# Output norms in steps behind later slots, and two more banks for the down units: a decoder layer on one Trainium2 core

## The chip, the cores and the metric

One core of one Trainium2 chip runs the kernel. Its engines are TensorE (PE, with its weight loads PEld), VectorE (DVE), ScalarE (ACT), GpSimd (POOL) and SyncE (SP); SP issues nearly all DMAs. The metric is device time in microseconds (us), the median of several runs. Before the change it is 2489.42 us, the median of 3 runs from 2483.08 to 2493.25.

## The reference

One layer of a decoder is computed for a prompt of 2048 positions and for 8 samples of 4 positions, all in float32, model width 1024:

```
z = rmsnorm(x) @ w_in                      # q, k, v for 8 heads; u, v for 8 gated groups
mix = [dilated window attention | u * spatial gate]
x = x + mix @ w_out
h = rmsnorm(x)
x = x + (silu(h @ w_gate) * (h @ w_up)) @ w_down      # hidden width 2816
y = rmsnorm(x)                                         # returned, with key and value windows
```

The change concerns the last two lines: the product with `w_down` and the final norm `y = x / sqrt(mean(x^2) + eps) * final_g`, which needs a whole row of 1024 values before any value of it can be scaled.

## The kernel before

The order of the instructions on every engine is the order in which the program writes them; nothing reorders them. A float32 product is made of three matmuls on a high and a low part of each operand (`hh*wh`, `hh*wl`, `hl*wh`), so each operand tile is first split: ACT copies the high part (L1883 and L1884), DVE subtracts it for the low part (L1885 and L1886).

The prompt's 16 row tiles of 128 go through the first half of the layer in three blocks of 6, 6 and 4 tiles. The hidden width is 22 slices of 128. Behind each block stand **down units** (`first_downs` L1785, `down_unit` L1780): the products of the last two slices with `w_down`, for one row tile each, in two halves of 512 columns and six matmuls a half (L1776). Each half fills a PSUM bank, and DVE adds that bank to the row tile (L1778, L1799). Before the change all units take their banks from `ps_o`, which hands out two banks by turns; `ps_t` hands out two others, used for transposes and gates elsewhere. Behind the units come the next block's products with `w_out` and its norm.

The other 20 slices of `w_down` are multiplied at the end, in the **second part** (class `Down`). They form 10 pairs (NJ), and the product is done as a seven-product block scheme in two halves of the rows (`hv` 0 and 1). Each product `s` (0 to 6) runs over the 10 pairs `j`, and one step `n` of these 2 x 7 x 10 = 140 is called a **slot**: `n = 70 hv + 10 s + j`. A slot has 12 matmuls of 512 columns, for four row groups `m` into four banks. Its program text, in order: `tick()` (work that `later(k, ...)` put k slots on), operand sums of slot n+3 on DVE (only for products 1 to 5), the split of slot n+3 on ACT and DVE, the loads of slot n+6 on SP, the matmuls, and in slots j = 0 to 3 the eviction (L1920) of one bank of the product before into the row tiles `acc[i]`. Operand tiles are a ring of 8 (two a slot), so the split of slot n+3 can start when the matmuls of slot n-1 are done. Weight tiles are a ring of 10. SP issues in order too: a store that waits for its row holds up the loads behind it. The last three slots (TAIL) are done at the end in the order of the row groups: for each `m` the 9 matmuls of slots 137 to 139, then its eviction.

Which half rows are finished when follows from `EVICTS`: the even row tiles get their first 512 columns complete with product 1 and the rest with product 5, the odd ones their second 512 columns with product 4 and the rest with product 6. So the **final norms** come in three places: for even rows behind product 5 (evicted from slots 60 and 130 on), for odd rows of `hv` 0 behind product 6 (from slot 70 on), for odd rows of `hv` 1 in the tail. `final_a` (L1808) squares the whole row on ACT; one slot later `rms_b` (L1457, L1458) forms mean and root; two slots later `final_b` (L1815) does the Newton step (L146 to L150) and the scaling of the whole row on DVE (L1818); three slots later SP issues the store. These steps stand in `tick()`, ahead of the slot's own split. Only the odd rows of `hv` 1 have a prepared half: `square_half` (L1950) squares it and multiplies it by the gain on POOL (L1955).

Of the kernel before, what the change touches and what calls it, by code (L numbers as in the profile page):

```python
# [10 lines left out]
F32 = mybir.dt.float32  # L11
F32R = mybir.dt.float32r
AF = mybir.ActivationFunctionType
OP = mybir.AluOpType
# [52 lines left out]
def hymba_step(ctx: ExitStack, tc: tile.TileContext, A: dict, O: dict):  # L67
# [26 lines left out]
    def ps_o():  # L94
        turn[1] ^= 1
        return bank(2 + turn[1])
# [81 lines left out]
    def zn_tile():  # L178
        return rp.tile([P, 512], F32, name="zn", tag="zn", bufs=3)
# [1597 lines left out]
                          stop=(z == FC - 1 and y == len(pairs) - 1))  # L1777
        dve.tensor_add(B.acc[i][0:nr, cs], B.acc[i][0:nr, cs], ps[0:nr])  # L1778

    def down_unit(B, i, h):  # L1780
        tick()
        for half in range(2):
            down_half(B, i, h, half, ps_o())

    def first_downs(B, i0, i1, h):  # L1785

# [39 lines left out]
    class Down:  # L1826
# [92 lines left out]
            x = self.acc[hv * 8 + 2 * m + q][:, cs]  # L1919
            dve.tensor_add(x, x, banks[m])  # L1920

        def final(self, i):
            final_a(self.acc[i], O["yp"][i * P:(i + 1) * P, :])

        def run(self):
            for n in range(2 * NS - TAIL):
                hv, s, j = self.at(n)
                tick()
                self.sums(n + 3)
                self.split(n + 3)  # L1930
                self.load(n + 6)
                if s in (0, 2) and j in (5, 8):
                    self.acc_loads(hv, s // 2, j // 8)
                if s > 2 and n % 2 == 0 and n < NS + 5 * NJ:
                    roll(1)
                self.mats(n)
                if n >= NJ and j < 4:
                    phv, ps_, _ = self.at(n - j - 1)
                    self.evict(phv, ps_, j, self.prev)
# [10 lines left out]
        def square_half(self, m):  # L1950

            x = self.acc[8 + 2 * m + 1][:, 512:]
            self.sq[m] = s1 = self.p2.tile([P, 4], F32, name="sq", tag="sq", bufs=4)
            act.activation(zn_tile(), x, AF.Square, accum_out=s1[:, 3:4])
            pool.tensor_mul(x, x, gain[1][:, 512:])  # L1955

        def tail(self):
            n0 = 2 * NS - TAIL
            for _ in range(4):
                tick()  # L1960

            def finish(m):
                i = 8 + 2 * m + 1
                x, s1 = self.acc[i], self.sq[m]
                rms_b(s1, P, s1[:, 3:4])
                r = rms_c(s1, P)
                act.activation(x[:, 512:], x[:, 512:], AF.Copy, scale=r)
                dve.scalar_tensor_tensor(x[:, 0:512], x[:, 0:512], r, gain[1][:, 0:512], op0=OP.mult, op1=OP.mult)
                for z in (1, 0):
                    sync.dma_start(O["yp"][i * P:(i + 1) * P, z * 512:(z + 1) * 512], x[:, z * 512:(z + 1) * 512])  # L1970
# [262 lines left out]
    for bi, B in enumerate(blocks):  # L2233
# [188 lines left out]
```

## Time and profile before

The profiled execution took 2493.14 us, with a span of 2491.4 us from the first to the last instruction; the median of the runs is 2489.42.

| engine | busy, us | share of the span |
|---|---|---|
| PE | 2397.9 | 96% |
| PEld | 2120.8 | 85% |
| DVE | 1691.0 | 68% |
| ACT | 1211.9 | 49% |
| POOL | 1183.7 | 48% |

How to read it: PE's busy time is a union of overlapping matmuls, so what counts is how far apart their starts are. The second part's matmuls start 0.227 us apart when nothing holds them, 2.72 us a slot. A row of the timeline gives start, length (us), engine, line, operation, the tiles written and read, the count where rows were merged, and in brackets how long the engine was idle before it and what ended that. Tile names are cut: `op` are split operands, `ac` and `acc` row tiles, `ps_m`, `ps_t`, `ps_o` banks, `fr` weight tiles.

### The profile page before, as it was taken

The page shows a single profiled execution, that of the slowest core. Times are in us where ns is not written, and L with a number is a line of the kernel's source. Part 1 is how long each engine was busy: PE and PEld are TensorE (multiplying, and loading weights), DVE is VectorE, ACT ScalarE, POOL GpSimd, SP SyncE. Part 2 cuts the span into 40 slices and gives each one's busy share as a digit, 9 for nine tenths or more (in the row PEclk, how much of TensorE's full clock was granted, in tenths as well). Part 3 has the DMA queues.
Part 4 walks back from the last instruction along what each step waited for, and adds up shares of the span by engine and source line. Part 5 has one row for each costly group of instructions (what it writes and reads, how often), then busy time and mean ns, then how long its engine had stood idle before and what let it go on. Part 6 is the DMA issues. An engine that isn't in the chain of part 4 may idle for free. (4 is left out here: it accounts for less than half of the span.)

```text
span 2491.4 us, 39127 instructions
## 1 busy us (share of the span) xinstructions
PE 2397.9 (96%) x13358; PEld 2120.8 (85%) x13358; DVE 1691.0 (68%) x3081; ACT 1211.9 (49%) x2385; POOL 1183.7 (48%) x909
## 2 busy tenths in 40 slices
PE   8999999999989889999999999999999999999997
PEld 6787777778888777999998899999799998887886
DVE  4368686446878777656655776776566666877876
ACT  6414344546877656433333633334455554445444
POOL 1145643224575746666663576666467881000000
PEclk9999999999999999999999999999999999999999
DMA  8863854788788665566659177666647776755832
GB/s 265 255 202 112 275 147 140 246 278 265 232 281 259 218 185 171 190 212 207 202 200 320 36 250 255 231 243 226 255 151 229 234 221 235 279 186 197 318 128 89
DMA packets 315221, 537.17 MB, mean 216 GB/s; under 512 B 28417, under 2 KB 151714, under 8 KB 309134
## 3 DMA queue, kind: packets, MB, share of 16 engines
q1 hardware_dynamic: 310060, 526.16, 64.6%
q10 hardware_dynamic: 4962, 8.51, 1.3%
q8 instruction: 106, 1.74, 0.3%
q14 instruction: 93, 0.76, 0.1%
HBM read 418.41 MB, written 186.28 MB: 243 GB/s over the span
## 5 line engine op out<-in xcount | busy, mean ns | idle before, releaser
L1686 PE MATMUL ps_m<-xh,op 128*128 128x384 f32 (+5 forms) x1932 | 612.3, 317 | 0.8 <-DVE raw L1714 0.5
L1687 PE MATMUL ps_m<-xl,op 128*128 128x384 f32 (+5 forms) x1932 | 612.0, 317 | 0.0
L1688 PE MATMUL ps_m<-xh,op 128*128 128x384 f32 (+5 forms) x1932 | 611.3, 316 | 0.0
L1623 POOL TENSOR_TENSOR op<-fr,op 128x512 fp32r<-128x512 f32 x286 | 402.6, 1424 | 91.7 <-ACT op L1619 65.0
L1686 PEld LDWEIGHTS ps_m<-xh,op 128*128 128x128 f32 x1932 | 363.9, 188 | 2.4 <-issue 0.8
L1687 PEld LDWEIGHTS ps_m<-xl,op 128*128 128x128 f32 x1932 | 363.8, 188 | 0.6
L1688 PEld LDWEIGHTS ps_m<-xh,op 128*128 128x128 f32 x1932 | 364.2, 188 | 0.0
L1623 POOL TENSOR_TENSOR op<-pair,op 128x512 fp32r<-128x512 f32 x126 | 169.6, 1347 | 158.3 <-DVE hr L1748 87.1
L1619 ACT ACTIVATE op<-fr 128x512 fp32r<-128x512 f32 x330 | 196.6, 621 | 12.2 <-PE ps_m L1438 6.0
L335 PE MATMUL ps_s<-wh,xh 128*128 128x512 f32 x480 | 195.8, 408 | 6.1 <-ACT xh L139 6.1
L336 PE MATMUL ps_s<-wl,xh 128*128 128x512 f32 x480 | 189.9, 396 | 0.0
L337 PE MATMUL ps_s<-wh,xl 128*128 128x512 f32 x480 | 189.5, 395 | 0.1
L1737 ACT ACTIVATE ps_t<-zn 128x384 f32<-128x384 f32 (+2 forms) x132 | 60.0, 454 | 250.4 <-DVE zn L1716 205.5
L1883 ACT ACTIVATE op<-fr 128x512 fp32r<-128x512 f32 x140 | 88.3, 631 | 173.9 <-issue 89.2
L1955 POOL TENSOR_TENSOR ac<-ac,final_g 128x512 f32<-128x512 f32 x2 | 2.6, 1296 | 351.9 <-DMA fr<-t_d 349.3
L1885 DVE TENSOR_TENSOR op<-fr,op 128x512 fp32r<-128x512 f32 x140 | 99.3, 710 | 80.4 <-ACT op L1883 80.1
L1619 ACT ACTIVATE op<-pair 128x512 fp32r<-128x512 f32 x126 | 79.0, 627 | 110.9 <-DVE pair L1609 110.9
L335 PEld LDWEIGHTS ps_s<-wh,xh 128*128 128x128 f32 x480 | 91.5, 191 | 34.5 <-issue 7.3
L1900 PE MATMUL ps_m<-op 128*128 128x512 f32 x280 | 109.0, 389 | 0.9 <-ACT op L1884 0.9
L1902 PE MATMUL ps_m<-op 128*128 128x512 f32 x280 | 109.1, 390 | 0.2
L337 PEld LDWEIGHTS ps_s<-wh,xl 128*128 128x128 f32 x480 | 91.5, 191 | 20.8 <-POOL xl L142 0.5
L1901 PE MATMUL ps_m<-op 128*128 128x512 f32 x280 | 109.0, 389 | 0.0
(551 smaller groups left out, 5942.0 us busy)
## 6 DMA issues: line engine op xcount, KB each, us to landing
fr<-in_w_gate_dram SPq DMA_DIRECT2D x132, 256.0 KB
out_ks_dram<-in_cache_k_dram SPq DMA_DIRECT2D x56, 512.0 KB
out_vs_dram<-in_cache_v_dram SPq DMA_DIRECT2D x56, 512.0 KB
fr<-in_w_up_dram SPq DMA_DIRECT2D x110, 256.0 KB
fr<-ab_d SPq DMA_DIRECT2D x88, 256.0 KB
a<-h_d SPq DMA_DIRECT2D x80, 256.0 KB
fr<-t_d SPq DMA_DIRECT2D x80, 256.0 KB
raw<-in_w_in_dram SPq DMA_DIRECT2D x72, 256.0 KB
```

Source lines behind the costliest of these rows:

```text
L335: pe.matmul(o[j], xh[:, k, :], wh, start=(k == 0), stop=False)
L336: pe.matmul(o[j], xh[:, k, :], wl, start=False, stop=False)
L337: pe.matmul(o[j], xl[:, k, :], wh, start=False, stop=(k == KD - 1))
L1619: act.activation(ops[f, j][0], ab[f][j], AF.Copy)
L1623: (eng or pool).tensor_sub(lo_, ab[f][j], hi.bitcast(F32))
L1686: pe.matmul(out, wh[:, ks], xh[:, :, k], start=(k == 0), stop=False)
L1687: pe.matmul(out, wh[:, ks], xl[:, :, k], start=False, stop=False)
L1688: pe.matmul(out, wl[:, ks], xh[:, :, k], start=False, stop=(k == 3))
L1885: dve.tensor_sub(wl, w, wh.bitcast(F32))
L1900: pe.matmul(banks[m], hh[:, ts], wh, start=first, stop=False, skip_group_check=more)
L1901: pe.matmul(banks[m], hh[:, ts], wl, start=False, stop=False, skip_group_check=more)
L1902: pe.matmul(banks[m], hl[:, ts], wh, start=False, stop=j == NJ - 1, skip_group_check=more)
```

## The change

Four things change.

1. Down units behind blocks 0 and 1 take their banks from `ps_t` and `ps_o` by turns; in front of the second part the units of the sample rows and of tile 3 take `ps_t`, the one of tile 2 `ps_o`.
2. Evictions: in all products but the last one of `hv` 1 they are written in slots j = 0, 2, 4, 6 instead of 0, 1, 2, 3.
3. Final norms: each row tile's first finished half is prepared early (`early_half`, behind products 1 and 4): one slot after its eviction ACT squares it and POOL multiplies it by the gain. Behind products 5 and 6 (`late_half`) six steps follow at the ends of later slots, 1 to 6 slots on: square of the other half (ACT), mean (DVE), root (ACT), Newton step and scaling of the half (DVE), scaling of the prepared half by a copy (ACT), two stores of a half row each (SP). In the last product of `hv` 1 the steps are 1, 2, 2, 3, 3, 4 slots on, with evictions in slots j = 0 to 3.
4. Tail: steps still queued are written out ahead of its matmuls; mean, root and Newton step of group m-1 stand ahead of the eviction of group m instead of behind it.

```diff
--- before.py
+++ after.py
@@ down units @@
-    def down_unit(B, i, h):
+    def down_unit(B, i, h, place=None):
         tick()
         for half in range(2):
-            down_half(B, i, h, half, ps_o())
+            down_half(B, i, h, half, (place or ps_o)())
@@ in class Down @@
-        def final(self, i):
-            final_a(self.acc[i], O["yp"][i * P:(i + 1) * P, :])
+        def behind(self, k, fn, *args):
+            self.queue.setdefault(self.n + k, []).append((fn, args))
+
+        def square(self, i, c):
+            x = self.acc[i][:, c * 512:(c + 1) * 512]
+            act.activation(zn_tile(), x, AF.Square, accum_out=self.sq[i][:, (0, 3)[c == i % 2]:][:, 0:1])
+
+        def early_half(self, i):
+
+            self.sq[i] = self.p2.tile([P, 4], F32, name="sq", tag="sq", bufs=8)
+            c = i % 2
+            x = self.acc[i][:, c * 512:(c + 1) * 512]
+            self.behind(1, self.square, i, c)
+            self.behind(1, pool.tensor_mul, x, x, gain[1][:, c * 512:(c + 1) * 512])
+
+        def late_half(self, i, quick=False):
+            steps = (1, 2, 2, 3, 3, 4) if quick else (1, 2, 3, 4, 5, 6)
+            for k, fn in zip(steps, (self.late_square, self.mean, self.root, self.scale, self.scale_rest, self.out)):
+                self.behind(k, fn, i)
+
+        def late_square(self, i):
+            self.square(i, 1 - i % 2)
+
+        def mean(self, i):
+            s1 = self.sq[i]
+            dve.tensor_scalar(s1[:, 0:1], s1[:, 0:1], s1[:, 3:4], None, op0=OP.add)
+            dve.tensor_scalar(s1[:, 1:2], s1[:, 0:1], 1.0 / D, EPS, op0=OP.mult, op1=OP.add)
+
+        def root(self, i):
+            act.activation(self.sq[i][:, 2:3], self.sq[i][:, 1:2], AF.Sqrt)
+
+        def scale(self, i):
+            r = rms_c(self.sq[i], P)
+            cs = slice((1 - i % 2) * 512, (2 - i % 2) * 512)
+            x = self.acc[i][:, cs]
+            dve.scalar_tensor_tensor(x, x, r, gain[1][:, cs], op0=OP.mult, op1=OP.mult)
+
+        def scale_rest(self, i):
+            x = self.acc[i][:, i % 2 * 512:(i % 2 + 1) * 512]
+            act.activation(x, x, AF.Copy, scale=self.sq[i][:, 2:3])
+
+        def out(self, i):
+            for c in (i % 2, 1 - i % 2):
+                cs = slice(c * 512, (c + 1) * 512)
+                sync.dma_start(O["yp"][i * P:(i + 1) * P, cs], self.acc[i][:, cs])
...
                 self.mats(n)
-                if n >= NJ and j < 4:
+                wide = not (hv and s == 6)
+                m = j // 2 if wide else j
+                if n >= NJ and m < 4 and not (wide and j % 2):
                     phv, ps_, _ = self.at(n - j - 1)
-                    self.evict(phv, ps_, j, self.prev)
-                    if ps_ == 5:
-                        self.final(phv * 8 + 2 * j)
-                    if ps_ == 6:
-                        self.final(phv * 8 + 2 * j + 1)
-                    if hv == 1 and s == 5:
-                        self.square_half(j)
+                    self.evict(phv, ps_, m, self.prev)
+                    i = phv * 8 + 2 * m
+                    if ps_ in (1, 4):
+                        self.early_half(i + ps_ // 4)
+                    elif ps_ in (5, 6):
+                        self.late_half(i + ps_ - 5, not wide)
+                for fn, args in self.queue.pop(n, ()):
+                    fn(*args)
...
         def tail(self):
             n0 = 2 * NS - TAIL
             for _ in range(4):
                 tick()
+            for n in sorted(self.queue):
+                for fn, args in self.queue[n]:
+                    fn(*args)
...
             for m in range(4):
                 for n in range(n0, 2 * NS):
                     self.mats(n, (m,))
+                if m:
+                    begin(m - 1)
+                    r[m - 1] = root_end(m - 1)
                 self.evict(1, 6, m, self.Y)
-                act.activation(zn_tile(), self.acc[8 + 2 * m + 1][:, 0:512], AF.Square, accum_out=self.sq[m][:, 0:1])
+                self.late_square(8 + 2 * m + 1)
                 if m:
-                    finish(m - 1)
-            finish(3)
+                    finish(m - 1, r[m - 1])
+            begin(3)
+            finish(3, root_end(3))
@@ in second_part: units of the sample rows and of tile 3; unit 2 stays @@
-        down_unit(B, m, h)
+        down_unit(B, m, h, ps_t)
...
-        down_unit(B, 3, h)
+        down_unit(B, 3, h, ps_t)
@@ behind blocks 0 and 1 @@
-            downs += [lambda B=B, pair=pair, i=i: down_unit(B, i, pair) for i in last[2:]]
+            downs += [lambda B=B, pair=pair, i=i, p_=p_: down_unit(B, i, pair, p_) for i, p_ in zip(last[2:], (ps_t, ps_o) * 2)]
```

On PE, the down units behind block 0 (`ps_o`, `ps_t` and `ps_m` are the kinds of banks, `dw` the weights, `hw` the hidden values):

```order
 L1797 MATMUL ps_m_14044<-dw,hw 128x512 x3
-L1776 MATMUL ps_o_14098<-dw,hw 128x512 x6
-L1776 MATMUL ps_o_14106<-dw,hw 128x512 x6
+L1776 MATMUL ps_t_14098<-dw,hw 128x512 x6
+L1776 MATMUL ps_t_14106<-dw,hw 128x512 x6
 L1776 MATMUL ps_o_14115<-dw,hw 128x512 x6
 L1776 MATMUL ps_o_14123<-dw,hw 128x512 x6
-L1776 MATMUL ps_o_14139<-dw,hw 128x512 x6
-L1776 MATMUL ps_o_14147<-dw,hw 128x512 x6
+L1776 MATMUL ps_t_14139<-dw,hw 128x512 x6
+L1776 MATMUL ps_t_14147<-dw,hw 128x512 x6
```

No matmul has moved; every second unit writes the other pair of banks.

On DVE, behind product 5 of `hv` 0, before the change (from a slot's split to the next slot's eviction; `s` holds a row's mean and root):

```order
L1885 TENSOR_TENSOR op<-fr_24073,op 128x512
L1886 TENSOR_TENSOR op<-a_23178,op 128x512
L1920 TENSOR_TENSOR ac<-ac,ps_o_23441 128x512
L146 RECIPROCAL s_24135<-s_24135 128x1
L148 TENSOR_SCALAR s_24135<-s_24135 128x1
L149 TENSOR_SCALAR s_24135<-s_24135 128x1
L150 TENSOR_SCALAR s_24135<-s_24135 128x1
L1818 SCALAR_TENSOR_TENSOR ac<-ac,s_24135,final_g 128x1024
L1457 TENSOR_SCALAR s_24167<-s_24167 128x1
L1885 TENSOR_TENSOR op<-fr_24093,op 128x512
L1886 TENSOR_TENSOR op<-a_23202,op 128x512
L1920 TENSOR_TENSOR ac<-ac,ps_o_23442 128x512
```

and in the changed program (`sq` holds mean and root):

```order
L1920 TENSOR_TENSOR ac<-ac,ps_o_23457 128x512
L146 RECIPROCAL sq<-sq 128x1
L148 TENSOR_SCALAR sq<-sq 128x1
L149 TENSOR_SCALAR sq<-sq 128x1
L150 TENSOR_SCALAR sq<-sq 128x1
L1957 SCALAR_TENSOR_TENSOR ac<-ac,sq,final_g 128x512
L1947 TENSOR_SCALAR sq<-sq 128x1
L1948 TENSOR_SCALAR sq<-sq 128x1
L1885 TENSOR_TENSOR op<-fr_24169,op 128x512
L1886 TENSOR_TENSOR op<-a_23255,op 128x512
L1885 TENSOR_TENSOR op<-fr_24193,op 128x512
L1886 TENSOR_TENSOR op<-a_23281,op 128x512
```

Between two evictions there are now two slots' splits instead of one, and the scaling is of half a row.

On ACT, in the last slots before the tail, before the change (L1811 squares a whole row, L1458 is the root, L1883 and L1884 are a slot's split):

```order
L1811 ACTIVATE pair,s_25868<-acc_18451 128x1024
L1458 ACTIVATE s_25868<-s_25868 128x1
L1883 ACTIVATE op<-fr_25796 128x512
L1884 ACTIVATE op<-a_24899 128x512
L1811 ACTIVATE pair,s_25900<-acc_18535 128x1024
L1458 ACTIVATE s_25900<-s_25900 128x1
```

and in the changed program (L1961 is the copy of the prepared half, L1951 the root, L1927 the square of half a row):

```order
L1961 ACTIVATE ac<-ac,sq 128x512
L1951 ACTIVATE sq<-sq 128x1
L1927 ACTIVATE zn,sq<-acc_18451 128x512
L1883 ACTIVATE op<-fr_25881 128x512
L1884 ACTIVATE op<-a_24973 128x512
L1961 ACTIVATE ac<-ac,sq 128x512
L1951 ACTIVATE sq<-sq 128x1
L1927 ACTIVATE zn,sq<-acc_18535 128x512
```

Root and square still stand between two slots' splits, now behind them in the program's slot, with a copy added.

More of the change, by code (lines that the diff above doesn't have):

```diff
@@ L1920, in evict @@
             dve.tensor_add(x, x, banks[m])
-        def final(self, i):
-            final_a(self.acc[i], O["yp"][i * P:(i + 1) * P, :])
+        def behind(self, k, fn, *args):
[33 more added lines that the diff above has]
+                sync.dma_start(O["yp"][i * P:(i + 1) * P, cs], self.acc[i][:, cs])
         def run(self):
+            self.queue = {}
             for n in range(2 * NS - TAIL):
+                self.n = n
                 hv, s, j = self.at(n)
@@ L1948, in run @@
             self.tail()
[L1950 to L1955, printed above, removed]
         def tail(self):
@@ L1960, in tail, with begin, root_end, finish @@
                 tick()
-            def finish(m):
+            for n in sorted(self.queue):
+                for fn, args in self.queue[n]:
+                    fn(*args)
+            def begin(m):
                 i = 8 + 2 * m + 1
-                x, s1 = self.acc[i], self.sq[m]
-                rms_b(s1, P, s1[:, 3:4])
-                r = rms_c(s1, P)
+                self.mean(i)
+                self.root(i)
+            def root_end(m):
+                return rms_c(self.sq[8 + 2 * m + 1], P)
+            def finish(m, r):
+                i = 8 + 2 * m + 1
+                x = self.acc[i]
                 act.activation(x[:, 512:], x[:, 512:], AF.Copy, scale=r)
                 dve.scalar_tensor_tensor(x[:, 0:512], x[:, 0:512], r, gain[1][:, 0:512], op0=OP.mult, op1=OP.mult)
-                for z in (1, 0):
-                    sync.dma_start(O["yp"][i * P:(i + 1) * P, z * 512:(z + 1) * 512], x[:, z * 512:(z + 1) * 512])
+                self.out(i)
+            r = {}
             for m in range(4):
```

## The prediction

> **What bounds the kernel now.** I read the stages first, then the starts of TensorE's matmuls, then what DVE and ACT do where those starts spread. The windows of the second part (us; then busy us of PE, PEld, DVE, ACT, POOL; granted clock; DMA share; GB/s):
>
> ```profile
> 2113.00:2250.00 137.00, 137.00 (x606) 113.46 (x605) 106.91 (x172) 58.96 (x102) 0.00 (x0) 1.00 0.64 218
> 2250.00:2306.00 56.00, 51.58 (x216) 39.88 (x216) 42.12 (x90) 28.97 (x59) 0.00 (x0) 1.00 0.67 226
> 2306.00:2440.00 134.00, 134.00 (x592) 110.96 (x591) 108.29 (x170) 58.94 (x106) 5.18 (x4) 1.00 0.60 212
> 2440.00:2475.00 35.00, 31.87 (x130) 24.96 (x129) 24.97 (x51) 17.14 (x35) 0.00 (x0) 0.95 0.19 70
> 2475.00:2491.40 16.40, 4.59 (x21) 3.46 (x19) 9.22 (x31) 5.54 (x14) 0.00 (x0) 0.79 0.34 128
> ```
>
> TensorE is full except in 2250-2306, in 2440-2475 and after it: where the norms of the output rows run. How much is lost there, from first matmuls of slots (0, 65, 76, 80):
>
> ```profile
> 2085.47 0.40 PE L1900 MATMUL ps_m<-op 128*128 128x512 f32 x1
> ...
> 2262.28 0.39 PE L1900 MATMUL ps_m<-op 128*128 128x512 f32 x1
> ...
> 2296.19 0.50 PE L1900 MATMUL ps_t<-op 128*128 128x512 f32 x1 [1.53 <-ACT op L1884]
> ...
> 2310.35 0.39 PE L1900 MATMUL ps_m<-op 128*128 128x512 f32 x1
> ```
>
> Slots 0 to 65 take 176.81 us, 2.72 each. The 15 slots from 65 to 80 take 48.07 where 40.80 would do: **7.27 us lost**. TensorE waits for split operands (ACT op). One norm slot on DVE, and ACT between:
>
> ```profile
> 2295.64 0.69 DVE L1885 TENSOR_TENSOR op<-fr,op 128x512 fp32r<-128x512 f32 x1 [0.79 <-ACT op L1883]
> ...
> 2296.86 0.68 DVE L1920 TENSOR_TENSOR ac<-ac,ps_m 128x512 f32<-128x512 f32 x1
> 2297.45 0.16 DVE L146 RECIPROCAL s<-s 128x1 f32<-128x1 f32 x1
> ...
> 2298.39 1.29 DVE L1818 SCALAR_TENSOR_TENSOR ac<-ac,s,final_g 128x1024 f32<-128x1024 f32 x1
> 2299.59 0.15 DVE L1457 TENSOR_SCALAR s<-s 128x1 f32<-128x1 f32 x1
> 2300.53 0.69 DVE L1885 TENSOR_TENSOR op<-fr,op 128x512 fp32r<-128x512 f32 x1 [0.79 <-ACT op L1883]
> ```
>
> ```profile
> 2299.77 0.20 ACT L1458 ACTIVATE s<-s 128x1 f32<-128x1 f32 x1 [0.99 <-DVE s L1457]
> 2299.88 0.61 ACT L1883 ACTIVATE op<-fr 128x512 fp32r<-128x512 f32 x1
> ```
>
> A closed ring: two subtractions 1.22, eviction 0.59, Newton 0.94, whole-row scaling 1.20, mean 0.15; then ACT's root, behind it ACT's next split (0.11 later), and 0.65 later DVE's next subtraction. Its period is 2300.53 - 2295.64 = 4.89 us against a slot of 2.72, so each norm slot eats 2.17 us of the lead that splitting has over TensorE. That lead in calm slots: the second row here is the last subtraction of slot 133's operands (the first is used further down).
>
> ```profile
> 2423.28 1.42 DVE L1885 TENSOR_TENSOR op<-fr,op 128x512 fp32r<-128x512 f32 x1 [0.72 <-ACT op L1883]
> ...
> 2447.83 0.68 DVE L1886 TENSOR_TENSOR op<-a,op 128x512 fp32r<-128x512 f32 x1
> ```
>
> It ends at 2448.51, and slot 133 starts at 2310.35 + 53 x 2.72 = 2454.5: a lead of 6.0 us.
>
> **The change: more banks for the down units.** These matmuls wait for DVE to empty a ps_o bank:
>
> ```profile
> 1320.19 2.96 PE L1776 MATMUL ps_o<-dw,hw 128*128 128x512 f32 x12
> 1323.72 5.87 PE L1776 MATMUL ps_o<-dw,hw 128*128 128x512 f32 x24 [0.57 <-DVE acc L1778]
> 1330.15 3.06 PE L1776 MATMUL ps_o<-dw,hw 128*128 128x512 f32 x12 [0.57 <-DVE acc L1778]
> ...
> 1749.47 2.84 PE L1776 MATMUL ps_o<-dw,hw 128*128 128x512 f32 x11 [0.57 <-DVE acc L1778]
> ...
> 2077.04 2.01 PE L1776 MATMUL ps_o<-dw,hs 128*64 128x512 f32 x8
> 2079.78 5.86 PE L1776 MATMUL ps_o<-dw,hw 128*128 128x512 f32 x24 [0.72 <-DVE acc L1778]
> ```
>
> Twelve matmuls from 1320.19 at 0.233 are through at 1322.99; the next starts at 1323.72: 0.73, and about 0.11 more on the first one after a stop. Three such waits and the longer one (2077.04 + 8 x 0.233 = 2078.90, start at 2079.78: 0.88 + 0.11) make 3 x 0.84 + 0.99 = **3.5 us**. With the units on two pairs of banks by turns, the pair wanted was last written two units earlier, at least 2.8 us ago, and DVE's order of evictions is the old one; the wait goes. What is late next is the bank of the first open unit, two units behind, with the same 2.8 us. The norms behind each block hang on TensorE's own banks, so they move with it. Value 3.5; bounds 2.0 (if the two later phases give part back) and 3.5.
>
> **The change: steps at the slots' ends (slots 60 to 82).** Evictions now come every second slot, and the steps behind them 1 to 6 slots later. DVE in an even slot: 1.22 + 0.59 + 0.94 + scaling of a half row + mean. The half-row scaling is 0.67 and mean to end of Newton 1.61, from the tail's rows:
>
> ```profile
> 2472.68 0.69 DVE L1920 TENSOR_TENSOR ac<-ac,ps_t 128x512 f32<-128x512 f32 x1 [0.88 <-PE ps_t L1902]
> ...
> 2484.48 0.75 DVE L1968 SCALAR_TENSOR_TENSOR acc<-acc,sq,final_g 128x512 f32<-128x512 f32 x1
> 2485.15 0.21 DVE L1456 TENSOR_SCALAR sq<-sq 128x1 f32<-128x1 f32 x1
> ...
> 2486.76 0.75 DVE L1968 SCALAR_TENSOR_TENSOR acc<-acc,sq,final_g 128x512 f32<-128x512 f32 x1
> ```
>
> The mean's two instructions are about 0.40 of that (1.61 less Newton's 0.94, 0.20 for the root and two hand-overs). So even slots cost 3.82, odd ones 1.22: 5.04 for two, against 5.44. From slot 77 the operand sums come back, 0.60 a slot; by then the evictions are over, and the worst pair is 3.64 + 1.61 + 0.40 = 5.65, once. On ACT an odd slot has split 1.04, copy about 0.62, root 0.11, half square 0.63: 2.40; an even one 1.04. The ring is open: what ACT needs in an odd slot DVE made in the slot before, and its split stands ahead of it. The 6.0 us of lead are hardly touched, and the 7.27 us go. I take 7.2; bounds 0 (the ring stays) and 7.27.
>
> The early halves are twelve more squares and twelve more POOL products. Their price on DVE shows in the row at 2423.28 above, 1.42 instead of 0.69, beside this POOL product:
>
> ```profile
> 2422.85 1.30 POOL L1955 TENSOR_TENSOR ac<-ac,final_g 128x512 f32<-128x512 f32 x1 [349.30 <-DMA fr<-t_d]
> ```
>
> That is 0.73 in an odd slot; POOL waits for ACT's square there, and nothing else is queued on POOL by then. Two slots then cost DVE 2 x 1.82 + 0.59 + 0.73 = 4.96 of 5.44: nothing on the path. Without the lead as cover it would be at most 12 x 0.73 = 8.8 us. Each of twelve 512 KB stores becomes two of 256 KB; with SP's 0.3 to 0.4 us an issue that is under 5 us of SP, which has no other work; see the third rival.
>
> **The change: the tail.** In the last seven slots (130 to 136, from 2310.35 + 50 x 2.72 = 2446.35) evictions come in every slot and the steps are packed, and there ACT's root still stands behind DVE's mean, and the next split behind root and square. I count from 2446.35. Slot 132's first subtraction is at 6.29 (slot start 5.44, ACT 0.20, 0.65); 1.22 + 0.59 + 0.40 brings 8.50; mean to root, root, half square and the next split's 0.65 are 0.04 + 0.11 + 0.63 + 0.65 = 1.43, so slot 133 subtracts at 9.93. Its ring is 1.22 + 0.59 + 0.94 + 0.67 + 0.40 + 1.43 = 5.25, slot 134's 4.66 (no eviction), slot 135's 4.03 (no square): 15.18, 19.84, 23.87. Then 1.22 + 0.94 + 0.67, and the last group's first eviction is at 26.70. Before, it is at 2472.68 - 2446.35 = 26.33: 0.4 later. From there the order inside a group decides: eviction to square 0.72, square read 0.76, mean to Newton 1.61, so the second eviction is at 29.79; with the copy of the half row (0.62) ahead of the root the next two are 3.15 apart, and the last scaling starts at 26.70 + 3.09 + 3 x 3.15 = 39.24. Before: 2486.76 - 2446.35 = 40.41. What follows it is unchanged. **Gain 1.2 us.** Bounds: if TensorE's last 36 matmuls are not held at all, the group's first eviction is at 7 x 2.72 + 2.04 = 21.1 and the gain is 6.8; if each of the eight steps has 0.3 more of hand-over, -1.2. I take 1.2, since the first rows of the ring are measured ones in another order.
>
> In that ring TensorE pauses for some 3 us before slot 136's split is through (it splits slot 139's operands), and the first of the four row groups ends about 25.5: 23.87 + 0.61 + 0.69, and the last product. What such a pause does shows here:
>
> ```profile
> 2470.04 0.50 PE L1901 MATMUL ps_t<-op 128*128 128x512 f32 x1 [2.01 <-DVE op L1885]
> ...
> 2471.11 0.63 PE L1900 MATMUL ps_t<-op 128*128 128x512 f32 x1
> 2471.54 0.63 PE L1901 MATMUL ps_t<-op 128*128 128x512 f32 x1
> ```
>
> After it the starts are 0.43 apart instead of 0.227, with a granted clock of 0.95 over that window; nine such matmuls, the second group, end at 25.5 + 3.9 = 29.4, before the eviction that wants them (29.79), so my sum has nothing for it. The Trainium skill, TensorE: Matmul & The Clock Gate, "What's actually happening", says that the array falls to half rate after an idle window of some 3.4 us and comes back after a busy one. The trace agrees with the halving, after less idle time. If by that rule all last 27 matmuls ran at half rate they would end at 25.5 + 11.5 = 37.0 instead of before the fourth eviction at 36.1, and 0.9 us of the tail's gain would go.
>
> **Sum:** 3.5 + 7.2 + 1.2 = 11.9 us off the profiled execution of 2493.14 us (span 2491.4 and 1.7 around it): 2481.2. The median of the three runs is 2489.42, 3.7 lower; the same 11.9 us give **2477.5 us**, -0.48%.
>
> **Rivals.** *The ring stays in part.* Speaks for it: every mean, root and scaling is still there, on the same engines in strict order. Against: a pair of slots would have to take 5.44 + 6.0 / 4 = 6.9 us to stall TensorE within a run of four, 1.9 more than counted. If the second run, which before started with some 3 us of lead, stalls by 4 us, the gain is 8: 2481.5.
>
> *The tail opens.* If scaling and roots fall into gaps that I count as ring, the gain is up to 3.5 + 7.2 + 6.8 = 17.5: 2472. For it: ACT is busy 17 of 35 us there. Against: order on ACT, as counted.
>
> *SP holds the loads back (slower).* SP issues in order, and the stores now wait for ACT's copy five slots behind the eviction. SP is held by such stores today, 6.6 us between these two rows:
>
> ```profile
> 2283.36 0.33 SPq L1842 DMA_DIRECT2D fr<-in_w_down_dram  x1
> 2289.93 0.34 SPq L1349 DMA_DIRECT2D out_yp_dram<-ac  x1
> ```
>
> The first store now stands before the load of slot 73, the last behind that of slot 88, so from slot 65's end to slot 87 these pass: eight stores (4.2 MB), loads of slots 73 to 90 (3.7 + 7.9 + 0.5 MB; the operands of product 1 take three tiles of 0.26 MB), two rows of x1 (1.05) and one cache piece (0.5): 17.8 MB in 22 x 2.72 - 2 = 57.8 us and at most 6.0 us of lead. It decides below 17.8 MB / 63.8 us = 279 GB/s.
>
> ```profile
> 2257.00:2290.00 33.00, 31.89 (x138) 25.36 (x137) 24.03 (x50) 16.22 (x33) 0.00 (x0) 1.00 0.77 263
> ...
> 2306.00:2338.00 32.00, 32.00 (x142) 26.47 (x141) 27.40 (x45) 14.20 (x25) 0.00 (x0) 1.00 1.05 386
> ```
>
> Loads alone run at 386; with stores and pieces 263 at a share of 0.77, some 340 if full. At 230 GB/s the bytes take 77.4 us, 13.6 too many, and the kernel ends at 2491, above today. I hold the rows' 340 for likelier.
>
> *The banks do nothing,* because the norm phase behind each block waits anyway: 8.4 us gained, 2481. Against: that phase starts from TensorE's own result.
>
> **Numbers.** Forecast with a gain of 9 to 14.5 us: 0.64. Ring in part 0.14, tail opens 0.11, SP 0.05, banks 0.06. The range from a gain of 17.5 with 3 us of run-to-run drift to a gain of 4 with as much leaves out SP's case and the ends: 2469 to 2489. A difference under 0.5%, 12.4 us, can hardly be told from none here, and the forecast lies just inside. Two fifths of its chance are beyond, with the opened tail 0.37 faster; 0.58 same; 0.05 slower.
>
> **What would show it.** Right: no matmul of slots 60 to 82 with a wait; slot 65 to 80 in 40.8 us; no wait at L1776; TensorE pausing before its last two slots, first eviction of the last group near 26.7 us after slot 130, last scaling near 39.2. Wrong: matmuls waiting for ACT op in slots 65 to 80 (ring), or with DMA named behind ACT's split in slots 75 to 88 (SP); new waits in the norm phases behind the blocks as long as those gone from L1776.

## The result and the profile after

| | median, us | lowest to highest | runs |
|---|---|---|---|
| before | 2492.82 | 2483.08 to 2498.76 | 20 |
| changed | 2479.52 | 2471.59 to 2487.26 | 20 |

The ratio is 0.9949, 95% interval 0.9939 to 0.9959: 0.51% faster, 13.3 us by the medians, where 11.9 were forecast. (The median of before has moved from 2489.42 with the seventeen runs that came in addition; the forecast of 2477.5 hung on the old one.)

The profiled execution of the changed kernel has a span of 2476.0 us, 15.37 less than that of before. Both programs have the same 13358 matmuls in the same order, so the two traces can be laid side by side matmul by matmul. The lead of the changed one grows like this: 3.36 us up to 1316 us, where nothing is changed yet (chance); 0.83, 0.85, 0.84 and 0.99 at the four places where before waits for a bank of the down units; 0.75 at 1443 us of before, a wait that the trace of before has and none of the other thirteen; -1.55 in a stretch near 1785 us with a halved clock, of which 0.3 comes back in a shorter wait behind it; 7.27 between slots 65 and 80; 1.69 from slot 130 to the end.

The down units behind block 0, and those in front of the second part (timeline of TensorE, changed kernel):

```profile
1319.63 2.96 PE L1776 MATMUL ps_o<-dw,hw 128*128 128x512 f32 x12
...
1325.23 2.96 PE L1776 MATMUL ps_o<-dw,hw 128*128 128x512 f32 x12
...
2073.47 2.96 PE L1776 MATMUL ps_o<-dw,hw 128*128 128x512 f32 x12
2076.26 2.96 PE L1776 MATMUL ps_t<-dw,hw 128*128 128x512 f32 x12
```

They start 2.80 us apart (from 1319.63 to 1325.23 in two steps; the unit between them writes `ps_t`), with no bracket behind them: no wait.

Starts of slots 65 and 80, and the windows of the second part (us; then busy us of PE, PEld, DVE, ACT, POOL; granted clock; DMA share; GB/s):

```profile
2255.87 0.39 PE L1900 MATMUL ps_m<-op 128*128 128x512 f32 x1
...
2296.67 0.39 PE L1900 MATMUL ps_m<-op 128*128 128x512 f32 x1
```

```profile
2255.87:2296.67 40.80, 40.80 (x181) 33.78 (x180) 34.67 (x87) 26.38 (x56) 0.00 (x0) 1.00 0.92 318
...
2432.67:2460.00 27.33, 24.09 (x98) 18.98 (x97) 19.03 (x47) 13.81 (x30) 0.00 (x0) 0.94 0.16 58
```

The fifteen slots take 40.80 us, 2.72 each, with TensorE full; the window from slot 130 on still has idle TensorE, 3.2 us of 27.3. One pair of norm slots on ACT, changed kernel (`issue` means that the profile shows nothing that ACT waited for):

```profile
2261.84 0.63 ACT L1883 ACTIVATE op<-fr 128x512 fp32r<-128x512 f32 x1 [1.84 <-issue]
...
2262.90 0.71 ACT L1961 ACTIVATE ac<-ac,sq 128x512 f32<-128x512 f32 x1
2263.51 0.19 ACT L1951 ACTIVATE sq<-sq 128x1 f32<-128x1 f32 x1
2263.60 0.62 ACT L1927 ACTIVATE zn<-ac 128x512 f32<-128x512 f32 x1
...
2264.28 0.64 ACT L1883 ACTIVATE op<-fr 128x512 fp32r<-128x512 f32 x1
```

Copy, root and square follow the split without a bracket: each finds its input ready, and the next split starts 2.44 us after the last one. Before, the root waited 0.99 us for DVE and the split stood behind it.

The tail still has its ring. First subtractions of the operands of slots 136 and 139, the last group's first eviction and the last scaling on DVE, changed kernel:

```profile
2442.64 0.69 DVE L1885 TENSOR_TENSOR op<-fr,op 128x512 fp32r<-128x512 f32 x1 [1.41 <-ACT op L1883]
...
2456.49 0.69 DVE L1885 TENSOR_TENSOR op<-fr,op 128x512 fp32r<-128x512 f32 x1 [0.79 <-ACT op L1883]
...
2459.31 0.68 DVE L1920 TENSOR_TENSOR ac<-ac,ps_t 128x512 f32<-128x512 f32 x1
...
2471.64 0.75 DVE L2018 SCALAR_TENSOR_TENSOR acc<-acc,sq,final_g 128x512 f32<-128x512 f32 x1
```

and TensorE there:

```profile
2453.83 0.50 PE L1902 MATMUL ps_t<-op 128*128 128x512 f32 x1
2457.03 0.79 PE L1900 MATMUL ps_t<-op 128*128 128x512 f32 x1 [2.70 <-ACT op L1884]
...
2459.75 0.47 PE L1900 MATMUL ps_t<-op 128*128 128x512 f32 x1
2460.06 0.40 PE L1901 MATMUL ps_t<-op 128*128 128x512 f32 x1
```

From 2453.83 to 2457.03 it stands still, and the matmuls that follow are 0.43 us apart up to 2459.75.

### The profile page after: what moved, and what is told of

It reads as the page before. It is cut to its first block, busy times and chain, and to the rows that moved or that the text cites. A ratio compares the mean times of both kernels' runs of the same rounds, so it can differ in the third digit from the quotient of the medians.

```text
span 2476.0 us, 39227 instructions
## 1 busy us (share of the span) xinstructions
PE 2394.6 (97%) x13358; PEld 2123.2 (86%) x13358; DVE 1694.0 (68%) x3093; ACT 1223.0 (49%) x2421; POOL 1209.2 (49%) x921
## 5 line engine op out<-in xcount | busy, mean ns | idle before, releaser
L1883 ACT ACTIVATE op<-fr 128x512 fp32r<-128x512 f32 x140 | 88.7, 634 | 181.7 <-issue 88.0
L1993 POOL TENSOR_TENSOR ac<-ac,final_g 128x512 f32<-128x512 f32 x12 | 19.5, 1622 | 319.6 <-ACT zn L1927 252.7
```

## The experiments

All twelve, with before and changed, in one table. "Lost" is the time from slot 65 to slot 130 less 65 x 2.72 = 176.8 us; the last three columns are counted from the start of slot 130, all from the profiled executions. "Half clock" says whether the stretch near 1785 us is there.

| kernel | median, us | ratio to before | lost, us | first eviction of the last group | last scaling | end | half clock |
|---|---|---|---|---|---|---|---|
| before | 2492.82 | 1 | 7.27 | 26.33 | 40.41 | 45.01 | no |
| changed | 2479.52 | 0.9949 (0.9939 to 0.9959) | 0.00 | 26.64 | 38.97 | 43.32 | yes |
| e1_banks | 2490.36 | 0.9989 (0.9976 to 1.0001) | 6.89 | 26.32 | 40.42 | 45.03 | yes |
| e2_norms | 2485.32 | 0.9966 (0.9952 to 0.9980) | 0.00 | 26.63 | 38.95 | 43.30 | no |
| e3_dense | 2479.76 | 0.9940 (0.9924 to 0.9957) | 0.00 | 26.63 | 38.95 | 43.30 | no |
| e4_packed | 2484.60 | 0.9959 (0.9945 to 0.9974) | 2.44 | 26.63 | 38.95 | 43.31 | yes |
| e5_root_later | 2488.96 | 0.9975 (0.9961 to 0.9990) | 2.26 | 25.10 | 39.33 | 43.93 | no |
| e6_tail_steps | 2474.00 | 0.9922 (0.9905 to 0.9939) | 0.00 | 22.50 | 34.83 | 39.18 | no |
| e7_tail_pipe | 2475.38 | 0.9927 (0.9910 to 0.9944) | 0.00 | 22.50 | 33.30 | 37.65 | yes |
| e8_tail_old | 2482.30 | 0.9952 (0.9938 to 0.9967) | 0.00 | 26.63 | 40.25 | 44.60 | yes |
| e9_more_dma | 2478.08 | 0.9950 (0.9931 to 0.9969) | 0.00 | 26.63 | 39.18 | 43.53 | no |
| e10_dense_packed | 2483.25 | 0.9965 (0.9951 to 0.9979) | 3.95 | 26.62 | 38.97 | 43.32 | yes |
| e11_whole | 2478.83 | 0.9951 (0.9936 to 0.9967) | 0.00 | 26.63 | 39.12 | 43.48 | no |
| e12_pair | 2473.41 | 0.9919 (0.9904 to 0.9934) | 0.00 | 22.50 | 32.38 | 37.43 | yes |

The ratios are good to some 0.15% (4 us), so most verdicts rest on the columns from the traces.

### The two halves of the change

e1_banks, the banks alone (the change's own lines on the kernel before):

> The kernel before with the change's banks for the down units alone. The prediction's term: the four waits at L1776 go (3.5 us), the ring behind slots 60 to 80 (7.3 us) and the tail stay as they are, so 2.5 to 3.5 us faster than before (0.10 to 0.14%). Rival, the banks do nothing: the same time as before within 0.5 us, with new waits of 0.7 to 0.9 us in the norm phases behind the blocks in place of those at L1776. A third possibility: after a pause of about 1.6 us in the norm phase of the third block the matmuls of the changed kernel start 0.43 us apart instead of 0.23 for nine of them (1783 to 1788 us of its trace), which costs 1.8 us; if the other banks bring that about, it is seen here too and the gain is 1.5 to 2.

e2_norms, all the rest without the banks:

> The changed kernel with the down units' banks as before: norms in steps, early halves, spaced evictions and the tail's new order. The prediction's terms: 7.3 us of ring and 1.2 to 1.7 us of tail, so 8.4 to 9 us faster than before, and 3.5 us slower than the change. No matmul of slots 60 to 82 waits; the four waits at L1776 are back. If the slowed stretch at 1783 us has nothing to do with the banks, it may appear here too.

e1 is 0.11% faster (interval 0.24% faster to 0.01% slower), 2.7 us; e2 is 0.34% faster, 8.5 us, with 8.4 to 9 expected; together 0.45, the change has 0.51. In e1's trace the four waits at L1776 are gone and none has come in the norm phases behind the blocks; the third possibility, the half clock, is there too. In time alone e1 can't be told from nothing. e2 has the four waits again, the first of them

```profile
1326.44 5.86 PE L1776 MATMUL ps_o<-dw,hw 128*128 128x512 f32 x24 [0.57 <-DVE acc L1778]
```

and loses nothing between slots 65 and 130. The rival "the banks do nothing" falls by the trace.

### What opened the ring

Three things changed there at once: the steps' distance, the evictions' distance, and half rows. e3_dense takes the second away:

```diff
-                m = j // 2 if wide else j
-                if n >= NJ and m < 4 and not (wide and j % 2):
+                m = j
+                if n >= NJ and m < 4:
```

> The changed kernel with evictions in slots j = 0, 1, 2, 3 of every product instead of 0, 2, 4, 6; the six steps stay a slot apart. Theory 1 (the ring is open because each step stands one slot behind the step that it needs): DVE has at most 3.82 us in a slot for two slots and 2.2 to 3.2 in the others, the lead of 6.0 us falls by 1 to 2 us, no matmul of slots 60 to 82 waits, and the time is that of the change within 0.7 us. Theory 2 (the ring is open because evictions are two slots apart): with evictions in every slot the 7.3 us come back at least in half: 3.5 us or more slower than the change.

e4_packed takes the first away:

```diff
-            steps = (1, 2, 2, 3, 3, 4) if quick else (1, 2, 3, 4, 5, 6)
+            steps = (1, 2, 2, 3, 3, 4)
```

> The changed kernel with the steps of all output norms packed as in the last product (1, 2, 2, 3, 3, 4 slots on), evictions still two slots apart outside the last product. Theory 1 (steps a slot apart open the ring): root waits for mean in the same slot and the copy for the Newton step, each ahead of the next split. Worked out from the rows of before: an odd slot 1.22 + 0.94 + 0.04 + 0.62 + 0.53 + 0.11 + 0.65 = 4.1 us, an even one 1.22 + 0.59 + 0.40 + 0.15 + 0.65 = 3.0; a pair 7.1 against 5.44. The first run of norms eats about 5.2 of the 6.0 us of lead, the second starts with some 2.6 and stalls TensorE by 2.5 to 4 us in slots 76 to 80: 2.5 to 4 us slower than the change. Theory 2 (the spacing of evictions opens it): no matmul waits in slots 60 to 82, the time is that of the change within 0.7 us.

e10_dense_packed takes both:

> The changed kernel with both: evictions in slots 0, 1, 2, 3 of every product and steps packed (1, 2, 2, 3, 3, 4 slots on). Theory 1 (packing alone closes the ring; density only adds DVE work): ring of 3.6, 5.25, 4.66, 4.0 and 3.4 us, 7.4 us eaten from 6.0, so TensorE loses about 1.4 us in the first run (slots 64 to 70) and 3 to 4 in the second: 4.5 to 5.5 us slower than the change, 2 more than packing alone. Theory 2 (packing costs the same with or without density): 2.5 us slower.

e11_whole keeps both and takes the half rows away in the first half of the rows (part of its edit):

```diff
+            if i < 8:
+                self.sq[i] = self.p2.tile([P, 4], F32, name="sq", tag="sq", bufs=8)
+                for k, fn in zip(steps, (self.whole_square, self.whole_mean, self.root, self.whole_scale, lambda i: None, self.out)):
+                    self.behind(k, fn, i)
+                return
...
-                    if ps_ in (1, 4):
+                    if ps_ in (1, 4) and phv:
```

> The changed kernel without early halves for the rows of the first half: these rows are squared and scaled as whole rows (1024 columns, ACT and DVE) in the same six places, evictions two slots apart. Theory (the steps' distance is what counts): a pair of slots costs DVE 2.44 + 0.59 + 0.94 + 1.20 + 0.15 = 5.32 us of 5.44, ACT's odd slot 1.04 + 1.04 + 0.11 = 2.2: the lead holds, no matmul of slots 60 to 82 waits, within 0.7 us of the change. From slot 77, with the operand sums, a pair costs 6.5 against 5.44, which the lead covers. Rival (halving the rows is needed): at least 2 us slower.

The loss is 0.00 in e3, 2.44 in e4, 3.95 in e10, 0.00 in e11. So the steps' distance opens the ring, and neither the spacing of the evictions nor the half rows are needed for it as long as the other is there; no run takes both away and leaves all six steps apart. Spaced evictions are worth 1.5 us where the steps are packed. e10 still loses 3.3 us less than before: that much comes from the half rows and from the steps' place behind the slot's split, and which of the two it is was not tested. In e4 the ring is closed again, one odd and one even slot on DVE:

```profile
2263.52 0.69 DVE L1885 TENSOR_TENSOR op<-fr,op 128x512 fp32r<-128x512 f32 x1 [0.79 <-ACT op L1883]
...
2267.62 0.69 DVE L1885 TENSOR_TENSOR op<-fr,op 128x512 fp32r<-128x512 f32 x1 [1.20 <-ACT op L1883]
...
2270.61 0.69 DVE L1885 TENSOR_TENSOR op<-fr,op 128x512 fp32r<-128x512 f32 x1 [0.79 <-ACT op L1883]
```

4.10 and 2.99 us, 4.1 and 3.0 expected; the first run of norms eats the lead down to 0.5 us without a wait, the second goes below zero. Half rows buy some lead, no time here: at its lowest the lead is 2.28 us in e11 and 3.86 in the changed kernel (both at slot 84, where the operand sums have come back). e10's 3.95 is less than the 4.5 to 5.5 expected, though more than e4's, as theory 1 has it.

### The least edit

e5_root_later moves only the root, and with it what follows it, in the kernel before:

```diff
-        later(1, rms_b, s1, n)
-        later(2, final_b, x, out, s1)
+        later(1, dve.tensor_scalar, s1[:n, 1:2], s1[:n, 0:1], 1.0 / D, EPS, OP.mult, OP.add)
+        later(2, act.activation, s1[:n, 2:3], s1[:n, 1:2], AF.Sqrt)
+        later(3, final_b, x, out, s1)
```

> The kernel before, with one thing changed in its final norms: the root stands one slot behind the mean (and Newton step, scaling and store one slot later too). Whole rows, evictions in every slot, no early halves, banks and tail as before. Theory: the ring of 4.89 us (mean, root, next split) is cut; what is left is eviction, square (1.04 and its read), root, next split: 1.22 + 0.59 + 1.95 = 3.76 us a slot at first, then DVE's own sum 0.94 + 1.20 + 0.15 + 1.22 + 0.59 = 4.10 once and 3.4 to 3.5 three times. Seven slots eat 6.6 us of 6.0, four calm ones give 3.3 back, the next seven eat 6.6 again: TensorE loses 0.6 + 3.3 = 3.9 us in slots 60 to 80 instead of 7.3, and the last product's norms open a little too: 3.5 to 5 us faster than before. Rival 1 (half rows and early halves are what opens it): 0 to 1 us faster. Rival 2 (the root's place is all of it): 7 us or more faster, no matmul of slots 60 to 80 waiting.

Between slots 65 and 130 it loses 2.26 us, so one slot between mean and root brings 5.0 of the 7.27; with 1.1 in the tail it comes to 6.1 in the trace and 0.25% (0.10 to 0.39) in time. Both rivals fall. The gain was expected at 3.5 to 5: the period in the full slots came as worked out (4.01 and 4.00 us; 4.10 expected; in this kernel the lines from the split on stand one further down, so L1886 is the first subtraction),

```profile
2285.96 0.69 DVE L1886 TENSOR_TENSOR op<-fr,op 128x512 fp32r<-128x512 f32 x1 [0.46 <-ACT op L1884]
...
2289.97 0.68 DVE L1886 TENSOR_TENSOR op<-fr,op 128x512 fp32r<-128x512 f32 x1
...
2293.97 0.68 DVE L1886 TENSOR_TENSOR op<-fr,op 128x512 fp32r<-128x512 f32 x1
```

but the first run ate 5.7 us, not 6.6, and the calm slots after it gave 4.1 back, not 3.3. What is left is DVE's own sum of a whole-row norm slot, and the square that stands between an eviction and the next split; in the changed kernel it stands behind that split.

### The tail

e6_tail_steps puts the last product's steps a slot apart as well:

```diff
-            steps = (1, 2, 2, 3, 3, 4) if quick else (1, 2, 3, 4, 5, 6)
+            steps = (1, 2, 3, 4, 5, 6)
```

> The changed kernel with the last product's six steps a slot apart too (1, 2, 3, 4, 5, 6 slots on), its evictions still in every slot; what is not done by slot 136 is written ahead of the tail's matmuls. Theory (the packed ring holds TensorE and the tail): DVE's own sum from slot 130 on is 1.81, 1.81, 2.21, 2.21 (under a slot of 2.72), then 3.23, 3.23, 2.83 and 1.61: the last group's first eviction at 22.7 us after slot 130's start instead of 26.6, TensorE without a wait before its last 36 matmuls and without the stretch of starts 0.43 us apart, the end 3.5 to 4 us earlier than the change's (0.15%). Rival (the tail is bound by DVE's work, which is the same and only stands later): within 0.7 us of the change.

e7_tail_pipe changes the order in the last groups in addition:

```diff
                 self.mats(n, (m,))
-                if m:
-                    begin(m - 1)
-                    r[m - 1] = root_end(m - 1)
                 self.evict(1, 6, m, self.Y)
                 self.late_square(8 + 2 * m + 1)
+                if m > 1:
+                    r[m - 2] = root_end(m - 2)
+                    finish(m - 2, r[m - 2])
                 if m:
-                    finish(m - 1, r[m - 1])
+                    begin(m - 1)
             begin(3)
+            finish(2, root_end(2))
             finish(3, root_end(3))
```

> The kernel of the run before in this set, and in the tail's groups DVE's next eviction and the next group's mean are written between a group's mean and its Newton step, so that squares and roots run beside them. Theory: the groups cost DVE its own 0.59 + 0.40 + 0.94 + 0.70 = 2.63 us each instead of 3.07 with the waits for square and root; last scaling some 10.2 us behind the first eviction instead of 12.3: 1.4 to 2 us off that kernel, 5 to 6 off the change. Rival (TensorE's groups, 2.04 us apart, or the last row's own chain set the end): no more than 0.7 us off that kernel.

e8_tail_old goes the other way, with the groups' order of before in the changed kernel:

> The changed kernel with the order of before inside the tail's groups: mean, root and Newton step of group m-1 behind the eviction and square of group m. Theory (the prediction's term): the groups go back from 3.07 us each to 3.5, and the last scaling starts 14.1 us behind the first eviction, as before, instead of 12.3: 1.5 to 1.8 us slower than the change; nothing else moves. Rival (the order is hidden by ACT's square and copy): within 0.5 us.

e6's first eviction stands at 22.50 (22.7 expected) and its end 4.14 us sooner (3.5 to 4 expected); TensorE has no wait from slot 130 to its last matmul (window from slot 130 on, 27.36 us busy of 27.36, clock 1.00):

```profile
2433.44:2460.80 27.36, 27.36 (x121) 22.33 (x119) 21.56 (x57) 15.57 (x36) 0.00 (x0) 1.00 0.21 77
```

So the packed ring held the tail, and the rival that DVE's work, the same in both, bounds it falls. e7 ends another 1.53 us sooner (1.4 to 2 expected), which its time, 1.4 us above e6's, is too coarse to show; e7's trace has the half clock and e6's hasn't. e8's last scaling is 1.28 later and its end too, somewhat less than the 1.5 to 1.8 expected: the order inside the groups gave the change 1.28 of its 1.69 us in the tail.

e12_pair is e7 with the last two row tiles' small operations on two columns (part of its edit):

```diff
+            s2 = self.sq_pair
+            dve.tensor_add(s2[:, 0:2], s2[:, 0:2], s2[:, 6:8])
+            dve.tensor_scalar(s2[:, 2:4], s2[:, 0:2], 1.0 / D, EPS, op0=OP.mult, op1=OP.add)
+            act.activation(s2[:, 4:6], s2[:, 2:4], AF.Sqrt)
+            newton(s2[:, 4:6], s2[:, 2:4])
```

> The kernel with steps a slot apart in the last product and the pipelined tail, and in addition mean, root and Newton step of the last two row tiles done together on two columns. Theory (DVE's own work sets the tail's end): mean 0.32 and Newton 0.94 fall away once, one more small instruction of about 0.2 and a wait for the root of about 0.3 come in: last scaling 0.6 to 1.0 us sooner, 32.3 to 32.7 us after slot 130's start instead of 33.3. In time that is 0.03%, below what the runs can tell. Against before: 18 to 19.5 us faster.

The last scaling is 0.92 us sooner, the end only 0.22: now the last stores stand in a row on SP, four of them from one stretch on (e7 first, then e12).

```profile
2468.09 2.42 SPq L1966 DMA_DIRECT2D out_yp_dram<-acc  x4
```

```profile
2473.32 1.79 SPq L1971 DMA_DIRECT2D out_yp_dram<-acc  x4
```

In e7 the four are spread by DVE's work over 2.42 us; in e12 they take 1.79, 0.45 each, from the moment the first is ready, so SP's issue holds up the last store: counted from slot 130 the row of stores ends at 34.92 in e7 and 34.31 in e12, 0.61 sooner of the 0.92. Another 0.39 goes behind the last issue, for which no run shows a cause. With a ratio of 0.9919 it is 0.81% (0.66 to 0.96) faster than before; e6, e7 and e12 can't be told apart in time. All three lie 4 to 6 us below the changed kernel in the medians, as in the column of the ends, though e7's interval overlaps the changed kernel's.

### The loads behind SP

e9_more_dma asks how near the third rival was:

```diff
-                if s > 2 and n % 2 == 0 and n < NS + 5 * NJ:
+                if n % 2 == 0 and 3 * NJ <= n < 9 * NJ:
                     roll(1)
```

> The changed kernel with the ten cache pieces that it copies in slots 100 to 118 copied in slots 70 to 88 instead: the same work, 5 MB more of DMA in the stretch where the stores of the first output rows hold SP. The third rival's account: 17.8 + 4.7 = 22.5 MB in 57.8 us and 6.0 us of lead, which asks for 353 GB/s. If 340 GB/s is what the queues give there (the prediction's reading), the bytes take 66.2 us and TensorE loses 2 to 4 us in slots 78 to 90, its matmuls waiting for splits that wait for DMA: 2 to 4 us slower than the change. If the rate goes on rising as in the changed kernel's trace (390 GB/s from 2285 to 2315 us), they take 57.7 us and nothing is lost: within 0.7 us of the change.

Nothing is lost, but ACT's splits now do wait for loads, in front of slot 89's for 3.60 us, and the lead falls to 1.99 us there:

```profile
2326.05 0.63 ACT L1883 ACTIVATE op<-fr 128x512 fp32r<-128x512 f32 x1 [3.60 <-DMA fr<-in_w_down_dram]
```

The queues gave 384 GB/s over 70 us,

```profile
2275.00:2345.00 70.00, 70.00 (x311) 57.99 (x310) 59.20 (x119) 37.64 (x74) 1.85 (x2) 1.00 1.03 384
```

with stores, loads and pieces mixed, not 340. With 5 MB more than the change moves there, a third of the lead was left.

## Why the prediction was right

**Banks, 3.5 us.** 3.51 in the traces. What was to be late next, the first open unit's bank, was not late.

**Steps, 7.2 us.** 7.27 between slots 65 and 80; e1, with the ring of before, loses 6.89 there, so the agreement to 0.1 us is partly luck. And the part gave two reasons in one breath: the pair of slots costs DVE 5.04 of the 5.44 us that it has, and the ring is open. The second one decides: e3 has evictions in every slot and e11 whole rows, and neither loses anything, since the lead of 6.0 us covers what their slots cost. That the first one is idle is not shown: e5 has whole rows in every slot, 4.00 us of DVE's own work each, and still loses 2.26.

**Early halves, nothing.** Their POOL products took longer than the 1.30 us read from before (group of POOL's instructions of the second part, changed kernel):

```profile
L1993 POOL TENSOR_TENSOR ac<-ac,final_g 128x512 f32<-128x512 f32 x12 | 19.5, 1622 | 319.6 <-ACT zn L1927 252.7 <-DMA fr<-t_d 63.1 <-DVE op L1886 3.8
```

1.62 us on average; the lead in the slots behind products 1 and 4 fell from 6.0 to no less than 5.3, as some of DVE's subtractions beside them took up to 1.35 us instead of 0.69. The price was on no path, as said; e11, which has none of them for the first half of the rows, takes the same time.

**Tail, 1.2 us.** 1.69. Counted from slot 130 the ring's subtractions were forecast at 9.93, 15.18, 19.84 and 23.87, the first eviction at 26.70 and the last scaling at 39.24; they stand at 9.97, 15.19, 19.81, 23.82, 26.64 and 38.97 (2442.64, 2456.49, 2459.31 and 2471.64 above are four of them, less 2432.67). The term that was a little off is the groups' distance, 3.15 forecast and 3.06 to 3.07 measured (the copy doesn't delay the root as much as counted), and 0.25 us came from behind the last scaling, which the sum left alone. TensorE's pause in front of slot 139 came, 2.97 us long; but six matmuls ran at half rate, not the nine counted, and not the 27 of the reading by the rule of the Trainium skill that the prediction weighed beside it. (By that rule, as the prediction itself gives it, the rate comes back after a busy window; the 27 did not follow from it.)

**The rivals.** *The ring stays in part* is what e4 made on purpose (2.44 us). *The tail opens* did not come by itself; e6 shows that it was there to be had: its end is 5.8 us sooner than before's, of the 6.8 given as the bound, 4.1 of them beyond the change. (DVE works without a break up to the first eviction of the last group, at 22.50 instead of the bound's 21.1.) *SP holds the loads back* did not come. The rate of 340 GB/s held against it was too low: it was worked out from a window in which the queues stood at a share of 0.77, and full they give 374 (2275 to 2315 us of the changed kernel) to 384 here, far above the 279 GB/s below which the rival would have decided. *The banks do nothing* falls by e1 and e2.

**The time.** The gain was forecast at 11.9 us and measured at 13.3 (10.2 to 15.2 by the interval). The traces' own account without chance is 3.51 + 7.27 + 1.69 = 12.5. The 2477.5 was counted from a median of three runs that lies 3.4 us under the median of twenty; the gain counted 1.4 us too small makes up for part of that in the time, by luck.

## What to carry to other kernels

When two engines hand a small value back and forth (mean, root, scaling) and one of them also prepares operands in strict order, put one period of other work between each step and the next; moving the root, and what follows it, by a slot brought 5.0 of 7.3 us, and the fuller rearrangement the rest. With the steps apart, either halving the work or spacing it could be taken away at no cost, as long as the lead of 6 us covered it. Measure the lead of the preparing engine over the consuming one slot by slot: what a run of slots eats of it, and what calm slots give back, foretold each stall here to within 1.7 us. The same packed ring cost 4.1 us in the last slots, where it runs once (e6), and 3.95 in the middle, where it runs twice (e10); my reading is that at the end no calm slots come to pay it back.

## What the runs showed of the hardware

Near 1785 us TensorE has a pause of the same length in the traces of the changed kernel and of before, and of these two only the changed kernel's runs at half rate behind it (timeline of the changed kernel, then of before; windows of 3.5 us behind the pause, where the granted clock stands third from the right):

```profile
1782.70 0.68 PE L1500 MATMUL ps_t<-ident,xns 32*128 32x32 f32 x8 [1.41 <-ACT xns L1488]
...
1784.58 0.63 PE L1437 MATMUL ps_o<-woh,xh 128*128 128x512 f32 x1
1785.00 0.63 PE L1438 MATMUL ps_o<-woh,xl 128*128 128x512 f32 x1
```

```profile
1789.36 0.68 PE L1500 MATMUL ps_t<-ident,xns 32*128 32x32 f32 x8 [1.41 <-ACT xns L1488]
...
1790.78 0.40 PE L1436 MATMUL ps_o<-woh,xh 128*128 128x512 f32 x1
1791.02 0.39 PE L1437 MATMUL ps_o<-woh,xh 128*128 128x512 f32 x1
```

```profile
1783.90:1787.40 3.50, 3.50 (x10) 2.75 (x9) 2.26 (x13) 2.52 (x10) 3.50 (x4) 0.52 0.40 108
```

```profile
1790.55:1794.05 3.50, 3.50 (x17) 2.82 (x16) 2.24 (x12) 2.53 (x10) 3.50 (x4) 1.00 0.38 109
```

The granted clock is 0.52 against 1.00, and it cost this execution some 1.5 us. Seven of the fourteen traces have this stretch, though the pause is 1.4 us long in all of them. In each trace the ends of all slow stretches lie on one grid (all but the last one, which the end of the program cuts off). In the changed kernel the last slow matmuls of three of them start at

```profile
148.74 0.55 PE L335 MATMUL ps_s<-wh,xh 128*128 128x512 f32 x1
...
1787.13 0.55 PE L1437 MATMUL ps_o<-wol,xh 128*128 128x512 f32 x1
```

and at 2459.75 (quoted above): 1638.39 and 672.62 us apart, 480.0 and 197.1 times 3.413 us. The Trainium skill, TensorE: Matmul & The Clock Gate, "What's actually happening", gives that window, 3413 ns, and calls it free-running; the traces agree with the length. They do not agree with an idle window of that whole length as the condition for the drop: here it follows a pause of 1.4 us and eight small transposes. Pause and transposes take 2.02 us together. Read on that grid, the slow stretch came in the seven traces where at least 1.94 of these lay in one window, and not in the other seven, where the window's edge left 1.91 or less on either side (e6 is one of them, though its pause by itself lay in one window). Since no run set the place of the grid, this is a reading of fourteen traces and not shown by an experiment. By it the half clock near 1785 us belongs to the draw of an execution: four of the eleven traces with the new banks are without it. All three with the old banks are without it too, so that the banks have no part in it is likely and not shown. A pause of about 1.5 us near 1390 us, with eight larger transposes behind it, was followed by a slow stretch in none of the fourteen; the pauses of 2.01 to 2.70 us in the tail (by their brackets) were in each of the eleven traces that have one.
